# A hybrid decoder layer on one core: where weight rests, block sums of the merged tensor and filler products stand

## The chip, the core and the metric

The kernel runs on one core of a Trainium2 chip. The engines are TensorE (PE, with its weight loads as PEld), VectorE (DVE), ScalarE (ACT), GpSimd (POOL) and SyncE (SP), which issues the transfers. The metric is the device time of one execution in microseconds (us), as the median of several runs. Besides it there is one profiled execution, from which all rows below come; a row's first number is its start, counted from the start of the span.

## The reference

One layer with two token mixers side by side, 1024 tokens, width 1024, float32:

```python
h = rms_norm(x, norm_w); proj = h @ w_in          # 7440 columns, split into 11 pieces
o_a = sliding_window_attention(rope(q), rope(k), v, sinks) * silu(a_gate)   # 16 heads, window 128
y_a = o_a @ w_a_proj
o_b = rms_norm(gated_linear_attention(b_q, b_k, b_v, log_a)) * silu(b_gate) # 4 heads, chunks
y_b = o_b @ w_b_proj
merged = sigmoid(m_a) * y_a + sigmoid(m_b) * y_b
out = rms_norm(x + merged @ w_out, final_norm_w)
```

## The kernel before

Every large product is taken with both factors split in two: a high part, rounded to TensorE's fp32r format by a copy on ScalarE, and a rest, which is the raw value minus the high part. `split_w` (L114 to L116) does it for weights, the rest on GpSimd (tiles `wl`), and `split_block` (L904 to L906) for blocks of 128x512 of an activation, the rest on VectorE or GpSimd. A product is then three matmuls: high by high, rest by high, high by rest. `half_product` (its matmuls have the line L132) takes 4 x 3 = 12 of them, 128x512 each; `token_product` (L420) the same with 256 columns.

Several projections are taken as 2x2 block products with seven products instead of eight (`seven_products`): four sums of weight blocks, four sums of activation blocks (`t1` to `t4`), seven products and seven sums of results. In the results, `u` is product 1 copied from PSUM by ScalarE, and each later product is added to it from PSUM by VectorE (L451, L459 and their neighbours). It serves three places: the pairs of projections with `w_in`, the four sets with `w_b_proj`, whose results are merged at once with `y_a` and the gates (`merge`), and the output projection with `w_out`, in two halves.

In order of time the span has these stages. The input norm and the transposes (0 to about 110 us). The pairs of projections with `w_in` (110 to 408). The window attention (408 to 728). It has more work for TensorE than its own, and at its end three "fillers" are put, `m_tiles`, each a projection tile of one of the gates, 48 matmuls of 128x512. The linear attention of heads 0 and 1 (728 to 798, `gla(0)`), a chain of small steps (`gla_step`, 16 of them) in which the engines wait for each other; between the steps stand matmuls of one more filler, spread by the list `pace`, which says behind which step each third matmul may stand. The linear attention of heads 2 and 3 with the products for `y_a` between its steps in the same manner (798 to 888). The blocks of `o_b` (`block_sums`, then the two last ones) and the four sets with `w_b_proj` (from about 882 to 990). The blocks of `merged`, all in one `block_sums` behind the last merge, with the splits of blocks 0, 1, 4, 5 and 6 on GpSimd and those of 2 and 3 on VectorE (990 to 1030). Then the output projection, the residual, the final norm and the stores.

The order of the instructions on each engine is not written out. A scheduler that simulates the program's timeline sets it, under the dependencies, the buffers in each pool and the limits of `pace`. A pool is a region of SBUF that opens where the code opens it; `vr`, `vh` and `vl` are a linear attention step's values and their two parts, in the pool `hpv`, which opens behind the window attention. Transfers stand in the queue of SP in program order as the scheduler gives it, and a transfer that waits for a buffer holds up those behind it. The rotation of queries and keys exchanges halves by such transfers (`qs`).

Of the kernel before, what the change touches and what calls it, by code (L numbers as in the profile page):

```python
# [25 lines left out]
P = 128  # L26
# [43 lines left out]
def layer_kernel(ctx: ExitStack, tc: tile.TileContext, consts, x, positions, norm_w, w_in, a_sinks,  # L70
# [42 lines left out]

    def split_w(raw, h, l):  # L114
        nc.scalar.copy(h, raw)  # L115
        nc.gpsimd.tensor_sub(l, raw, h.bitcast(F32))  # L116
# [10 lines left out]
    def half_product(p, w, m, start, stop):  # L127

        for k in range(4):
            with tc.issue_after(pace.pop(0)) if pace else nullcontext():  # L130
                for y, (a, b) in enumerate(((w[0], m[0]), (w[0], m[1]), (w[1], m[0]))):
                    nc.tensor.matmul(p, a[:, k, :], b[:, k, :], start=start and k == 0 and y == 0,  # L132
                                     stop=stop and k == 3 and y == 2)
# [282 lines left out]
    def token_product(p, w, m, t):  # L416

        for k in range(4):
            for y, (i, j) in enumerate(((0, 0), (1, 0), (0, 1))):
                nc.tensor.matmul(p, m[i][:, k, t * P : t * P + P], w[j][:, k, :], start=k == 0 and y == 0,  # L420
                                 stop=k == 3 and y == 2)

    def seven_products(raw, tset, n, u_pool, dest, emit, early=None, fine=False):
# [6 lines left out]
        nb = n // P  # L430

        def product(raw, m):
            w = part(raw, n)
            x = [bank("sj") for b in range(nb)]
            for b in range(nb):
                if n == P:
                    half_product(x[b], w, m, True, True)
                else:
                    for t in range(2):
                        token_product(x[b][:, t * 256 : t * 256 + 256], w, m, 2 * b + t)  # L440
            return x
# [4 lines left out]
        def like(p, o):  # L446
            return p.rearrange("p (t c) -> p t c", t=2) if len(o.shape) == 3 else p

        def add(o, u, x):
            for b in range(nb):  # L450
                nc.vector.tensor_add(o[b], like(u[b], o[b]), like(x[b], o[b]))  # L451

        def earlier(u, a, th):
            for b in range(nb):
                if early:
                    early(u[b], a, th, b)

        def give(a, th, u, x):
            o = [dest(a, th, b) for b in range(nb)]  # L459
            for b in range(nb):  # L460
                nc.vector.tensor_add(o[b], like(u[b], o[b]), like(x[b], o[b]))
                emit(o[b], a, th, b)

        x = product(a11, b11)
        u = tiles("u")
        for b in range(nb):
            nc.scalar.copy(u[b], x[b])  # L467
        x = product(a12, b21)
        c = [dest(0, 0, b) for b in range(nb)]
        add(c, u, x)  # L470
        earlier(c, 0, 0)
        for b in range(nb):
            emit(c[b], 0, 0, b)
        x = product(a22, t4)
        c = [dest(1, 0, b) for b in range(nb)]
        for b in range(nb):
            nc.scalar.copy(c[b], like(x[b], c[b]))
        earlier(c, 1, 0)
        nc.vector.tensor_add(a22, a21, a22)
        nc.vector.tensor_sub(a21, a11, a21)  # L480
        nc.vector.tensor_sub(a11, a22, a11)
        nc.vector.tensor_sub(a12, a12, a11)
        add(u, u, product(a11, t2))
        u3 = tiles("u3")
        add(u3, u, product(a21, t3))
        for b in range(nb):
            nc.vector.tensor_add(c[b], c[b], like(u3[b], c[b]))
            emit(c[b], 1, 0, b)
        x = product(a22, t1)
        add(u, u, x)  # L490
        earlier(u3, 1, 1)
        give(1, 1, u3, x)
        earlier(u, 0, 1)
        if not fine:
            give(0, 1, u, product(a12, b22))
            return
        w = part(a12, n)
        for b in range(nb):
# [569 lines left out]
```

## Time and profile before

| | |
|---|---|
| median of three runs | 1111.57 us (1110.83 to 1113.48) |
| profiled execution, own time | 1108.61 us |
| its span | 1106.7 us |
| mean granted TensorE clock | 0.979 |
| PE busy | 1027.7 us, 93% |
| PEld busy | 873.9 us, 79% |
| DVE busy | 774.7 us, 70% |
| ACT busy | 542.4 us, 49% |
| POOL busy | 684.3 us, 62% |

Busy time is the time in which an instruction runs, and a share is over the whole span; stages with different limits are mixed in it. A row of the chain of waits is a start, a length and what filled it. In a row of stretches stand the length, then busy time and count of instructions for PE, PEld, DVE, ACT and POOL, then the granted clock, the share of DMA and GB/s. A row of groups has the line, engine, operation, result and inputs, count, busy time and mean ns of one, and the idle time ahead of it with what ended it.

### The profile page before, as it was taken

The page shows a single profiled execution, that of the slowest core. Times are in us where ns is not written, and L with a number is a line of the kernel's source. Part 1 is how long each engine was busy: PE and PEld are TensorE (multiplying, and loading weights), DVE is VectorE, ACT ScalarE, POOL GpSimd, SP SyncE. Part 2 cuts the span into 40 slices and gives each one's busy share as a digit, 9 for nine tenths or more (in the row PEclk, how much of TensorE's full clock was granted, in tenths as well). Part 3 has the DMA queues.
Part 4 walks back from the last instruction along what each step waited for, and adds up shares of the span by engine and source line. Part 5 has one row for each costly group of instructions (what it writes and reads, how often), then busy time and mean ns, then how long its engine had stood idle before and what let it go on. Part 6 is the DMA issues. An engine that isn't in the chain of part 4 may idle for free.

```text
span 1106.7 us, 16321 instructions
## 1 busy us (share of the span) xinstructions
PE 1027.7 (93%) x5544; PEld 873.9 (79%) x5544; DVE 774.7 (70%) x1241; ACT 542.4 (49%) x1312; POOL 684.3 (62%) x542
## 2 busy tenths in 40 slices
PE   4999999899999999999999999988999997994896
PEld 3786787688889997888888878777788886873896
DVE  5999887335564323489788788748755299899766
ACT  6345865333342214556666666557654143243444
POOL 6033555777985446578677567747744246688685
PEclk9999999999999999999999999989999998996999
DMA  7332443452424152222222124266644587531315
GB/s 256 87 114 68 144 160 119 142 188 95 131 98 127 65 153 60 65 69 68 68 83 78 49 77 132 82 206 206 219 148 152 194 253 238 171 115 57 124 50 190
DMA packets 126403, 141.07 MB, mean 127 GB/s; under 512 B 10352, under 2 KB 87024, under 8 KB 126320
## 3 DMA queue, kind: packets, MB, share of 16 engines
q1 hardware_dynamic: 126320, 140.03, 40.5%
q8 instruction: 44, 0.72, 0.3%
q14 instruction: 39, 0.32, 0.1%
HBM read 95.04 MB, written 40.24 MB: 122 GB/s over the span
## 4 chain that ended last, share of the span: by engine, by line
PE 60%; DVE 16%; POOL 8%; issue 6%; ACT 6%; DMA 4%; SPq 1%; POOLq 0%; DVEq 0%; ACTq 0%
PE pj L132 22%; PE sj L132 15%; PE sj L420 11%; POOL wl L116 3%; PE sc L689 2%; PE av L729 2%; PE av L774 2%; POOL b L906 2%; DMA r<-sp_ob 1%; POOL o L906 1%; ACT wh L115 1%; PE pt L713 1%; PE sc L774 1%; DVE u L523 1%; DMA gt<-sp_cum 1%
## 5 line engine op out<-in xcount | busy, mean ns | idle before, releaser
L132 PE MATMUL pj<-o,wh 128*128 128x512 f32 x1088 | 353.6, 400 | 2.5 <-ACT o L204 1.9
L132 PEld LDWEIGHTS pj<-o,wh 128*128 128x128 f32 x1088 | 200.8, 190 | 44.2 <-ACT o L204 2.1
L116 POOL TENSOR_TENSOR wl<-wr,wh 128x1024 fp32r<-128x1024 f32 (+1 forms) x76 | 167.4, 2211 | 107.5 <-ACT wh L115 99.7
L116 POOL TENSOR_TENSOR wl<-sraw,wh 128x512 fp32r<-128x512 f32 (+1 forms) x98 | 155.3, 1600 | 107.6 <-ACT wh L115 105.5
L132 PE MATMUL pj<-o,wl 128*128 128x512 f32 x544 | 215.6, 396 | 0.0
L132 PEld LDWEIGHTS pj<-o,wl 128*128 128x128 f32 x544 | 102.5, 188 | 21.6
L115 ACT CAST wh<-wr 128x1024 fp32r<-128x1024 f32 (+1 forms) x76 | 66.9, 890 | 93.3 <-PE pj L132 23.9
L132 PE MATMUL sj<-o,wh 128*128 128x512 f32 x352 | 110.5, 395 | 0.7 <-ACT u L467 0.7
L451 DVE TENSOR_TENSOR u<-u,sj 128x512 f32<-128x512 f32 x72 | 49.2, 683 | 72.0 <-PE sj L420 40.5
L115 ACT CAST wh<-sraw 128x512 fp32r<-128x512 f32 (+1 forms) x98 | 63.2, 678 | 57.2 <-PE sj L420 29.1
L420 PE MATMUL sj<-wh,b 128*128 128x256 f32 x320 | 62.2, 296 | 21.7 <-ACT b L905 14.7
L132 PEld LDWEIGHTS sj<-o,wh 128*128 128x128 f32 x352 | 65.9, 187 | 16.9 <-ACT u L467 1.1
L420 PEld LDWEIGHTS sj<-wh,b 128*128 128x128 f32 x320 | 52.8, 203 | 23.1 <-ACT b L905 15.1
L132 PE MATMUL sj<-o,wl 128*128 128x512 f32 x176 | 69.4, 394 | 0.0
L721 POOL TENSOR_TENSOR ch<-ph,cst 128x512 fp32r<-128x512 f32 x32 | 38.4, 1201 | 48.4 <-ACT ph L720 36.0
L704 ACT ACTIVATE sm<-sc,nm 128x129 f32<-128x129 f32 x128 | 45.8, 368 | 37.4 <-DVE nm L700 36.4
L132 PE MATMUL sj<-b,wh 128*128 128x512 f32 x160 | 51.0, 402 | 5.6 <-ACT wh L115 5.6
L420 PE MATMUL sj<-wh,o 128*128 128x256 f32 x320 | 55.2, 277 | 0.1
L420 PEld LDWEIGHTS sj<-wh,o 128*128 128x128 f32 x320 | 48.4, 188 | 0.4 <-ACT wh L115 0.3
L420 PE MATMUL sj<-wl,b 128*128 128x256 f32 x160 | 45.8, 293 | 0.2 <-POOL wl L116 0.2
L609 POOL TENSOR_TENSOR qs<-qs,sin 128x512 f32<-128x512 f32 x18 | 25.4, 1409 | 31.0 <-DMA qs<-q 31.0
L420 PE MATMUL sj<-wl,o 128*128 128x256 f32 x160 | 44.3, 277 | 0.0
(314 smaller groups left out, 2737.3 us busy)
## 6 DMA issues: line engine op xcount, KB each, us to landing
sraw<-in_w_in_dram SPq DMA_DIRECT2D x32, 512.0 KB, 4.0
wr<-in_w_in_dram SPq DMA_DIRECT2D x26, 512.0 KB, 4.0
r<-sp_ob SPq DMA_DIRECT2D x28, 256.0 KB, 4.3
qs<-q SPq DMA_DIRECT2D x72, 64.0 KB, 2.0
xt<-in_x_dram SPq DMA_DIRECT2D x8, 512.0 KB, 8.6
sp_ma<-gt SPq DMA_DIRECT2D x16, 256.0 KB, 2.0
sp_mb<-c SPq DMA_DIRECT2D x16, 256.0 KB, 2.0
gt<-sp_cum SPq DMA_DIRECT2D x16, 256.0 KB, 3.7
```

Source lines behind the costliest of these rows:

```text
L115: nc.scalar.copy(h, raw)
L116: nc.gpsimd.tensor_sub(l, raw, h.bitcast(F32))
L132: nc.tensor.matmul(p, a[:, k, :], b[:, k, :], start=start and k == 0 and y == 0, stop=stop and k == 3 and y == 2)
L420: nc.tensor.matmul(p, m[i][:, k, t * P : t * P + P], w[j][:, k, :], start=k == 0 and y == 0, stop=k == 3 and y == 2)
L451: nc.vector.tensor_add(o[b], like(u[b], o[b]), like(x[b], o[b]))
L609: nc.gpsimd.tensor_mul(qs, qs, sin[:, sl])
L689: nc.tensor.matmul(s[:, h * 256 : h * 256 + 256], lq, kk[kv][x][:, k0 : k0 + 2, :].rearrange("p n t -> p (n t)"), start=x == 0, stop=x == 1)
L704: nc.scalar.activation(sm[:, j, :], sel[j // 2][:, j % 2, :], AF.Exp, bias=nm[:, j : j + 1], accum_out=den[:, j : j + 1])
L721: nc.gpsimd.tensor_mul(ch, ph.bitcast(F32), leb)
L729: nc.tensor.matmul(av[:, b * 256 : b * 256 + 256], val[:, blk, kv, :], part[:, 2 * b : 2 * b + 2, :], start=y == 0, stop=y == len(terms) - 1)
L774: nc.tensor.matmul(p, a[i], b[j], start=start and y == 0, stop=stop and y == 2)
L906: (eng or nc.vector).tensor_sub(m[1][:, k, :], r, f(m, 0, k))
```

## The change

1. `split_w` takes its engine from a list, `rest`. It is GpSimd as before until the first three tiles of `y_a`, and VectorE from there on.
2. `seven_products` is written anew. Weight parts of products 1, 2 and 6 and the sums of weights stand at its start, later weight parts ahead of the product that uses them. Without `order` (the pairs with `w_in`) the sums are as before, and product 6 is copied to a tile of its own. With `order`, products 3 and 5 are accumulated on product 1's bank in PSUM and product 7 on product 4's, with copies of the bank in between on ScalarE (`u1`, `u3`, `u5`); VectorE then adds four times per block instead of seven.
3. The pool `hpv` opens ahead of the window attention. Two of the fillers stand at the attention's end instead of three, two in the linear attention's first half instead of one, and `pace` lets six of their matmuls stand behind each step instead of three.
4. `block_sums` is gone. The first five blocks of `o_b` are taken row by row ahead of the later `y_a` tiles, the last two behind products of the first set with `w_b_proj`. The differences of `merged` are taken for the first three of its four rows behind each set, and the splits stand behind the products of the last set. All of this is on VectorE.
5. In the output projection the two halves of `w_out`'s rows are exchanged, the order of the products is (1, 2, 4, 6, 3, 5, 7) in the first half and (1, 2, 6, 3, 5, 4, 7) in the second, the residual is added behind the sum for three of four blocks, and the multiplication by the final norm's weights goes from GpSimd to VectorE.

```diff
+    rest = [nc.gpsimd]
     def split_w(raw, h, l):
         nc.scalar.copy(h, raw)
-        nc.gpsimd.tensor_sub(l, raw, h.bitcast(F32))
+        rest[0].tensor_sub(l, raw, h.bitcast(F32))
...
-    def seven_products(raw, tset, n, u_pool, dest, emit, early=None, fine=False):
+    def seven_products(raw, tset, n, u_pool, dest, emit, order=None, early=None, fine=False, after=None):
...
+        w = {i: part(r, n) for i, r in ((1, a11), (2, a12), (6, a22))}
         nc.vector.tensor_add(a22, a21, a22)
         nc.vector.tensor_sub(a21, a11, a21)
         nc.vector.tensor_sub(a11, a22, a11)
         nc.vector.tensor_sub(a12, a12, a11)
...
+        for i in order:
+            ahead(i)
+            x[i] = x[{3: 1, 5: 1, 7: 4}[i]] if i in (3, 5, 7) else [bank("sj") for b in range(nb)]
...
+            for b in range(nb):
+                product(i, b)
+            if i in (1, 3, 5):
+                u[i] = [u_pool.tile([P, 512], F32, name=f"u{i}") for b in range(nb)]
+                for b in range(nb):
+                    nc.scalar.copy(u[i][b], x[i][b])
...
+            if i == 2:
+                give(0, 0, 1, 2)
+            if i in (4, 5) and 4 in x and 5 in u:
+                give(1, 1, 5, 4)
+            if i in (5, 6) and 6 in x and 5 in u:
+                give(1, 0, 5, 6)
+            if i == 7:
+                give(0, 1, 3, 7)
+            if after:
+                after(i)
...
+    c3 = ExitStack()
+    hpv = c3.enter_context(pool_of(name="hpv", bufs=4))
     with ExitStack() as c2:
...
-                for _ in range(3):
+                for _ in range(2):
                     m_tiles([fillers.pop(0)])
...
-    pace += [steps[min(15, 2 + i)] for i in range(16 * len(fillers))]
+    pace += [steps[min(15, 2 + i // 2)] for i in range(16 * len(fillers))]
...
     ya_tiles((0, 1, 2))
+    rest[0] = nc.vector
...
+    def sum_row(k):
+        t1s.append(c21[3] if k == 3 else rp.tile([P, 512], F32, name="r"))
+        t2s.append(rp.tile([P, 512], F32, name="r"))
+        nc.vector.tensor_sub(t1s[k], c22[k], c21[k])
+        if k < 3:
+            less_row(k)
+
+    def less_row(k):
+        nc.vector.tensor_sub(t2s[k], c12[k], t1s[k])
+        nc.vector.tensor_sub(c22[k], c12[k], c22[k])
+
+    def sums(i):
+        y = {1: 0, 2: 1, 3: 3, 4: 5, 5: 4, 6: 2, 7: 6}[i]
+        mt[y] = block(y)
+        rows = {0: c21, 1: c11, 2: c11, 3: t2s, 4: c22, 5: t1s}
+        if i < 7:
+            for k in range(4 if i == 2 else 3):
+                split_block(mt[y], k, rows[y][k])
...
         seven_products([[r[:, 4 * i : 4 * i + 4, :] for r in w] for i in range(2)], ob, P, up_,
-                       lambda a, th, b: mg[a][th][:, k, :], merge)
+                       lambda a, th, b: mg[a][th][:, k, :], merge, range(1, 8), after={0: last_blocks, 3: sums}.get(k))
+        if k < 3:
+            sum_row(k)
...
-    mt = blocks() + last_blocks()
-    block_sums(mt, [(k, [mg[i][th][:, k, :] for i in range(2) for th in range(TH)]) for k in range(4)], zw, (0, 1, 4, 5, 6))
...
-            nc.sync.dma_start(w[i, a], w_out[i * 512 : i * 512 + 512, c : c + 256].rearrange("(k p) c -> p k c", p=P))
+            nc.sync.dma_start(w[i, a], w_out[512 - i * 512 : 1024 - i * 512, c : c + 256].rearrange("(k p) c -> p k c", p=P))
...
-                    nc.gpsimd.tensor_mul(o[:, t, :], o[:, t, :], fnw[:, cs])
+                    nc.vector.tensor_mul(o[:, t, :], o[:, t, :], fnw[:, cs])
```

The scheduler makes of it another order on the engines. In the first place below, TensorE's rows before, between two steps of the linear attention's heads 0 and 1, `pj` is the filler, L813 to L815 are a step's first three products, and `sc` is the update of a state.

```order
L847 MATMUL pt<-cst,on 128x128 x2
L813 MATMUL av<-bq,bk 128x64
L814 MATMUL av<-bq,bk 64x64
L815 MATMUL av<-cst,kp 128x128
L132 MATMUL pj<-o_83,wh 128x512
L132 MATMUL pj<-o_84,wh 128x512
L132 MATMUL pj<-o_83,wl 128x512
L774 MATMUL sc<-vh,kth 128x256
```

Three filler matmuls stand between the first products of a step and its next ones. The same place on TensorE now, where L850 to L852 are a step's first products and the row behind the fillers is its inner product with the values:

```order
L884 MATMUL pt<-cst,on 128x128 x2
L850 MATMUL av<-bq,bk 128x64
L851 MATMUL av<-bq,bk 64x64
L852 MATMUL av<-cst,kp 128x128
L134 MATMUL pj<-o_85,wh 128x512
L134 MATMUL pj<-o_86,wh 128x512
L134 MATMUL pj<-o_85,wl 128x512
L134 MATMUL pj<-o_85,wh 128x512
L134 MATMUL pj<-o_86,wh 128x512
L134 MATMUL pj<-o_85,wl 128x512
L811 MATMUL av<-vh,ath 128x256
```

Three more filler matmuls have come into the gap; they stood at the window attention's end. The second place is GpSimd before, at the blocks of `merged` (`o_9494` to `o_9497` are the quarters of `merged`, the `b_` and the other `o_` tiles the parts of its blocks, `wl` weight rests):

```order
L906 TENSOR_TENSOR b_10123<-o_9494,b_10122 128x512 x3
L906 TENSOR_TENSOR b_10125<-o_9496,b_10124 128x512 x3
L906 TENSOR_TENSOR b_10123<-o_9494,b_10122 128x512
L116 TENSOR_TENSOR wl<-wr,wh 128x1024 x2
L906 TENSOR_TENSOR b_10131<-o_9495,b_10130 128x512 x3
L906 TENSOR_TENSOR o_10133<-o_9494,o_10132 128x512 x3
L906 TENSOR_TENSOR b_10125<-o_9496,b_10124 128x512
L116 TENSOR_TENSOR wl<-wr,wh 128x1024
L906 TENSOR_TENSOR o_10135<-o_9497,o_10134 128x512 x4
L906 TENSOR_TENSOR o_10133<-o_9494,o_10132 128x512
L906 TENSOR_TENSOR b_10131<-o_9495,b_10130 128x512
L116 TENSOR_TENSOR wl<-wr,wh 128x1024 x3
```

GpSimd did the rests of five blocks (L906) and weight rests of `w_out` (L116) in one piece here, behind the last weight rests of `w_b_proj`. Now no row of these stands on GpSimd, which has nothing between the linear attention's last rows and the sums of the final norm. The third place is VectorE now, in the last of the four sets with `w_b_proj` (L459 adds out of PSUM, L1052 and L1053 are the merge, L940 is a block's rest, L439 and L440 are sums of weights, L118 a weight rest):

```order
L459 TENSOR_TENSOR o_9468<-u_9925,sj 128x512
L459 TENSOR_TENSOR o_9467<-u_9925,sj 128x512
L118 TENSOR_TENSOR wl<-wr,wh 128x512
L439 TENSOR_TENSOR wr<-wr 128x512
L1052 SCALAR_TENSOR_TENSOR o_9468<-ym,o_9468 128x512
L1052 SCALAR_TENSOR_TENSOR o_9467<-ym,o_9467 128x512
L940 TENSOR_TENSOR b_10014<-o_9467,b_10013 128x512
L440 TENSOR_TENSOR wr<-wr 128x512
L940 TENSOR_TENSOR b_10014<-o_9467,b_10013 128x512
L459 TENSOR_TENSOR o_9465<-u_10011,sj 128x512
L1053 TENSOR_TENSOR o_9468<-o_9468,yt 128x512
L118 TENSOR_TENSOR wl<-wr,wh 128x512
```

Rests of `merged`'s blocks and weight rests now stand between the merges, in VectorE's own queue.

238 lines of the change are left out of this document (129 added, 109 removed).

## The prediction

> **What bounds the kernel now.** I read four views in this order: the chain of waits, the busy time by stretches, what TensorE waited for, and the timeline of the last stages. The chain first (start, length, what; all in us):
>
> ```profile
> 715.24 5.60 PE pj L132 x24
> ...
> 728.50 5.25 DMA vr<-sp_bv
> ...
> 775.00 4.88 DMA oraw<-sp_oa
> ...
> 1031.84 4.58 POOL wl L116
> 1036.46 47.41 PE sj L420 x398
> ```
>
> Outside a few places the chain is TensorE at its own pace: 24 matmuls of 512 columns take 5.60 us (0.233 us each), and 398 of 256 columns 47.41 us (0.119 us each). The places where it leaves TensorE are a value load at the start of the linear attention (728.50) and VectorE and GpSimd work before the output projection. The stretches show how much each is worth (length, then busy time and count of PE, PEld, DVE, ACT, POOL, granted clock, DMA):
>
> ```profile
> 711.00:728.00 17.00, 16.80 (x90) 13.67 (x90) 6.61 (x18) 8.60 (x22) 8.27 (x6) 1.00 0.32 109
> 728.00:798.40 70.40, 59.56 (x349) 50.27 (x348) 53.38 (x135) 45.55 (x144) 52.02 (x70) 0.93 0.69 222
> 798.40:888.60 90.20, 90.20 (x488) 75.61 (x487) 44.92 (x115) 38.50 (x107) 35.17 (x47) 1.00 0.54 173
> 888.60:990.30 101.70, 96.06 (x409) 77.93 (x409) 93.92 (x111) 38.80 (x66) 61.52 (x39) 0.97 0.64 200
> 990.30:1096.00 105.70, 83.67 (x661) 81.96 (x660) 83.40 (x93) 43.97 (x99) 82.81 (x59) 0.90 0.27 88
> ```
>
> TensorE idles 10.8 us in the linear attention's first half (728 to 798.4), nothing after it, 5.6 us in the products with w_b_proj, 22.0 us from the output projection's first matmul to the last one, and 10.7 us are behind its last matmul (1096 to 1106.7). What lies ahead of 711 keeps its order on TensorE. What it waits for in the third stage:
>
> ```profile
> PE sj L420 <- ACT b L905: 14.7, 2, 12.6
> ...
> PE sj L132 <- ACT wh L115: 5.6, 1, 5.6
> ```
>
> ACT L905 is the rounding of merged's blocks, which itself waits for VectorE. So the bound from 882 to 1032 is VectorE, and these stretches show how:
>
> ```profile
> 882.00:919.40 37.40, 31.83 (x138) 25.40 (x136) 36.58 (x49) 17.78 (x32) 14.97 (x9) 0.97 0.85 275
> 919.40:975.00 55.60, 55.54 (x234) 45.34 (x235) 48.64 (x61) 17.43 (x32) 34.31 (x22) 0.96 0.61 180
> 975.00:1019.40 44.40, 25.93 (x143) 22.27 (x142) 43.99 (x30) 17.32 (x30) 44.40 (x25) 0.85 0.26 89
> 1019.40:1032.00 12.60, 9.38 (x54) 8.97 (x54) 12.46 (x18) 5.01 (x8) 0.21 (x2) 0.77 0.01 2
> ```
>
> VectorE is busy 141.7 of 150.0 us. But with GpSimd busy all the time (975 to 1019.4) it does 30 instructions in 44 us, 1.47 us each; with GpSimd idle (1019.4 to 1032) 18 in 12.5 us, although four of these are twice as wide. Single rows say the same:
>
> ```profile
> 882.80 0.69 DVE L917 TENSOR_TENSOR r<-r 128x512 f32<-128x512 f32 x1
> 883.41 0.68 DVE L906 TENSOR_TENSOR b<-r,b 128x512 fp32r<-128x512 f32 x1
> ...
> 885.21 0.68 DVE L920 TENSOR_TENSOR r<-r,t 128x512 f32<-128x512 f32 x1
> ...
> 1009.88 1.75 DVE L917 TENSOR_TENSOR o<-o,o 128x512 f32<-128x512 f32 x1
> 1011.55 1.75 DVE L920 TENSOR_TENSOR o<-o,t 128x512 f32<-128x512 f32 x1
> ...
> 1028.80 0.68 DVE L906 TENSOR_TENSOR b<-o,b 128x512 fp32r<-128x512 f32 x1
> 1029.40 1.22 DVE L481 TENSOR_TENSOR wr<-wr 128x1024 f32<-128x1024 f32 x1
> 1030.54 1.27 DVE L451 TENSOR_TENSOR o<-u,sj 128x512 f32<-128x512 f32 x2
> ```
>
> ```profile
> 1009.37 8.40 POOL L906 TENSOR_TENSOR o<-o,o 128x512 fp32r<-128x512 f32 x5
> ```
>
> From 882.80 to 885.21 four instructions of 128x512 go by, one per 0.603 us (the next starts before the last one's 0.68 are over); at 1009.88, beside GpSimd's five, the same L917 takes 1.75. One of 128x1024 takes 1.14 us from start to start (1029.40 to 1030.54).
>
> **The change part by part.** (1) Linear attention: values early, a second filler. Today TensorE is full up to 728 (16.80 of 17.00) and then lacks work. One filler is 48 matmuls at 0.233 = 11.2 us; it leaves the full stretch and goes between the steps (six filler matmuls a step instead of three, 1.4 instead of 0.7 us, in the rows of the order shown with the change), and eight values are loaded and four of them split at about 410 us instead of 728, so that the wait at 728.50 (5.25 us) goes. All work is the same; what can be won is the idle time, 10.8 us, and a part of what the clock of 0.93 costs on 59.6 us (up to 4 us, if it comes from the gaps). Against all of it stands that VectorE is busy 53.38 of 70.40 us there and would have to do that in some 60, and that the load of 4.88 us at 775.00, on which ScalarE stands, stays. I take 10 us; bounds 0 and 14.
>
> (2) Differences and splits, VectorE alone. By the order of the changed kernel, from the first split of o_b to the last split of merged VectorE executes 191 instructions of 128x512 (56 splits, 28 weight rests, 16 adds out of PSUM, 32 merges, 16 + 4 differences of o_b, 16 of weights, 16 of merged, 7 others) and 9 of 128x1024. GpSimd, whose rows of the order are shown with the change, has none beside them. At the spacings above: 191 x 0.603 + 9 x 1.14 = 125.4 us. Before, the same stretch runs from VectorE's first L906 at 882.07 to the end of the last at 1029.48 (1028.80 + 0.68): 147.4 us, 8.3 of them idle in the four stretches. With the same idle time the new one takes 133.7, a gain of 13.7. This is longer than TensorE's own work of that stretch, so VectorE stays the bound, by less.
>
> ```profile
> 882.07 0.69 DVE L906 TENSOR_TENSOR b<-r,b 128x512 fp32r<-128x512 f32 x1 [3.72 <-ACT b L905]
> ```
>
> Behind the last split today TensorE needs 66.5 us to its last matmul at 1096, since it then still waits for GpSimd's 4.58 us of weights (1031.84). In the new order the split that comes last (t4, product 6) is followed by 11 products of 48 matmuls at 0.119 = 62.8 us, and their weights are split: 3.7 us more. Together 17.4 us. Bounds: without any idle time on VectorE 25.7; at the 0.69 us that a row lasts rather than 0.603, 191 x 0.69 + 9 x 1.22 + 8.3 = 151.1 us, and nothing is left (3.7 lost and 3.7 won).
>
> (3) Sums in PSUM. Three of seven adds fall away per product set (12 in the stretch, already left out of the 191), one more copy on ScalarE comes, at 38.80 of 101.7 us busy without weight. Products 3, 5 and 7 now wait until their bank was copied or read; product 2, 4 or 6 runs meanwhile (12 x 0.233 = 2.8 us, or 5.7 in the output projection), longer than a copy and an add: 0, and up to 2 us each where VectorE is late, which the idle time of (2) holds.
>
> (4) Weights ahead in the earlier products. On TensorE, ScalarE and GpSimd the order up to the attention differs only in names (a copy of product 6 goes to a tile of its own): 0, bounds -2 and 2.
>
> (5) Eight value loads and four splits at the attention's start. The loads go to SP's queue ahead of the exchanges for the rotation, and some of them wait for GpSimd's splits of the first, 25.9 / 32 = 0.81 us each by the group of these splits, so the exchanges stand behind them. Behind that group's row stands one from GpSimd's timeline at the attention's start:
>
> ```profile
> L769 POOL TENSOR_TENSOR vl<-vr,vh 128x256 fp32r<-128x256 f32 x32 | 25.9, 814 | 20.2 <-ACT vh L768 20.2
> ```
>
> ```profile
> 418.01 1.29 POOL L609 TENSOR_TENSOR qs<-qs,sin 128x512 f32<-128x512 f32 x1 [6.95 <-DMA qs<-q]
> ```
>
> GpSimd is idle 6.95 us there, which covers its four splits (3.3 us); the queue may be late by 1 to 3 us, and behind it stands the key path. I take a loss of 1, bounds 0 and 4.
>
> (6) The end. The multiplications by the norm's weights (24 of 128x256) and the weight rests go to VectorE: by the order it then has, from the last split of merged on, some 30 rows of 128x512 at 0.603, 14 of 128x1024 at 1.14 and 40 of 128x256 at 0.3 to 0.4 (half a 512's and its start), about 50 us under some 63 of TensorE, so TensorE stays the bound. The last 10.7 us (add, square, sum, reciprocal root on GpSimd, two multiplications, store) keep their steps: 0, bounds -2 and 2.
>
> **The rivals.** (a) VectorE's price is the row's length, 0.69, not the spacing: (2) gives nothing, 1106.7 - 10 + 1 = 1097.7. For it: chains of dependent instructions could not overlap; against it: the rows from 882.80 depend on each other in part and are still 0.603 apart. [...]
>
> (b) The linear attention gains nothing: it is bound by its chain over ScalarE, VectorE and GpSimd (45.55, 53.38 and 52.02 of 70.40), and the filler only fills the waits: then the 11.2 us that left the stretch before 728 are won and lost again in the steps, and the span is 1106.7 - 17.4 + 1 = 1090.3.
>
> (c) TensorE alone bounds: (1) 14, (2) 25.7, (5) 0: 1106.7 - 39.7 = 1067.
>
> (d) The slower one: VectorE's instructions are slow for another reason than GpSimd, such as the loads (DMA share 0.85 at 882), and keep the mean of 882 to 1019.4, 129.2 us / 140 = 0.92 us. Now that the weights and all splits stand in its queue, the stretch takes 191 x 0.92 + 9 x 1.74 + 8.3 = 199.7 us, 52.3 more: 1106.7 + 52.3 - 3.7 - 10 + 1 = 1146.3. It decides from 0.73 us per instruction on, where the loss in (2) eats the other gains. Against it: at 882.80 the loads are at their densest and the rows 0.603 apart. [...]
>
> **How the numbers follow.** 1106.7 - 10 - 17.4 + 1 = 1080.3 us of span. The median of the runs, 1111.57, stands 4.9 above the span of the profiled execution (its own time, 1108.61, 1.9 above it): 1085.2. With 4.9 on each: (a) 1102.6, (b) 1095.2, (c) 1071.9, (d) 1151.2. Chances: forecast 0.60, (a) 0.10, (b) 0.12, (c) 0.14, (d) 0.04. The forecast's own bounds, two terms at their ends at once being rare, are 1074 to 1097; to leave out no more than 2 in 10 the range takes in most of (c) and (a): 1068 to 1102. A measurement of this kernel tells 0.3%, 3.3 us, from no change: faster 0.93, same 0.03 (between (a) and (d)), slower 0.04.
>
> **What would show it.** After: GpSimd nearly empty from the first o_b split to the norm, VectorE rows of 128x512 at 0.6 to 0.7 us there and none at 1.7; that stretch 126 to 140 us long; no TensorE wait over 5 us at the output projection's start, and the granted clock near 1 there; TensorE's idle time in the linear attention's first half below 3 us, with no value load in the chain. It is wrong if VectorE's rows stay above 0.8 us, if idle time on it between 882 and the output projection grows beyond some 20 us (loads of merged's inputs or SP's queue late), or if the attention's start loses more than 4 us to the early values.

## The result

The changed kernel takes 1083.62 us in the median of four runs (1080.67 to 1085.99), the kernel before 1111.20 (four runs, 1110.33 to 1113.48): a ratio of 0.9747, 95% interval 0.9715 to 0.9779. The profiled execution of the changed kernel took 1085.99 us, the slowest of the four, with a span of 1084.2 and a granted clock of 0.988. A second set of runs gave 0.9734 (0.9709 to 0.9760), a median of 1081.58 and a profiled span of 1080.0.

The stretches of the changed kernel, cut where VectorE's first split of o_b begins (879.3), its last split of merged ends (1014.4) and the last matmul begins (1075.2); the columns are those of the stretches before:

```profile
711.00:728.00 17.00, 15.50 (x87) 12.34 (x86) 13.70 (x28) 6.59 (x19) 13.74 (x12) 1.00 0.30 98
728.00:798.40 70.40, 64.23 (x384) 54.31 (x382) 54.30 (x135) 49.07 (x150) 51.93 (x68) 0.98 0.76 246
798.40:879.30 80.90, 80.90 (x447) 68.05 (x446) 41.40 (x111) 33.82 (x98) 18.70 (x39) 1.00 0.47 151
879.30:1014.40 135.10, 126.00 (x613) 104.79 (x612) 126.94 (x202) 59.64 (x102) 0.00 (x0) 0.99 0.55 176
1014.40:1075.20 60.80, 60.21 (x510) 60.02 (x508) 46.26 (x83) 31.08 (x83) 3.73 (x10) 1.00 0.37 119
1075.20:1084.20 9.00, 0.26 (x3) 0.05 (x1) 3.46 (x11) 3.58 (x8) 3.48 (x7) 0.69 0.69 255
```

The same cuts in the kernel before:

```profile
882.10:1029.50 147.40, 120.11 (x553) 99.43 (x551) 139.14 (x152) 56.26 (x96) 93.72 (x55) 0.92 0.52 164
1029.50:1097.30 67.80, 67.42 (x555) 67.01 (x556) 45.64 (x64) 31.55 (x80) 54.45 (x43) 0.97 0.36 117
1097.30:1106.70 9.40, 0.31 (x3) 0.12 (x2) 3.87 (x14) 4.04 (x10) 3.22 (x8) 0.71 0.60 223
```

From the first split of o_b to the last of merged VectorE now does 202 instructions instead of 152 (the counts of these rows) in 12.3 us less, and GpSimd none instead of 55. A single instruction shows why. VectorE's timeline of the changed kernel at the end of that stretch:

```profile
1005.51 0.67 DVE L1011 TENSOR_TENSOR o<-o,o 128x512 f32<-128x512 f32 x1
1006.12 0.68 DVE L940 TENSOR_TENSOR o<-o,o 128x512 fp32r<-128x512 f32 x1
1006.72 1.21 DVE L439 TENSOR_TENSOR wr<-wr 128x1024 f32<-128x1024 f32 x1
...
1013.73 0.68 DVE L940 TENSOR_TENSOR b<-o,b 128x512 fp32r<-128x512 f32 x1
```

Nothing lasts 1.7 us there any more, and 128x512 follow each other by 0.60 us. Its chain of waits goes over to TensorE behind that:

```profile
1003.85 1.13 DVE wl L118
1006.79 1.13 DVE wr L439
1008.59 60.54 PE sj L422 x508
```

The 508 matmuls run without a break up to 1069.1; what the path holds behind them are the last adds and the final norm. What was lost stands at the other end, and the waits of TensorE show it (all of the program, longest first after the input norm's):

```profile
PE pt L684 <- ACT q L681: 4.2, 1, 4.2
...
PE sj L134 <- ACT wh L117: 0.9, 1, 0.9
```

The first of them, 4.2 us, is at the start of the window attention; before it was 0.9.

For the comparison of all runs I read four places out of each profiled execution: the first score product of the attention, VectorE's first split of o_b, the end of its last split of merged, and the start of the last matmul. Between them lie the stages (us; the first column is a point in time, the others lengths):

| kernel | first score | to first o_b split | to last split of merged | to last matmul | behind it | span |
|---|---|---|---|---|---|---|
| before | 456.3 | 425.8 | 147.4 | 67.8 | 9.4 | 1106.7 |
| changed | 463.0 | 416.3 | 135.1 | 60.8 | 9.0 | 1084.2 |
| changed, again | 461.6 | 411.4 | 137.3 | 60.8 | 9.0 | 1080.0 |
| late values | 457.9 | 411.0 | 136.2 | 60.8 | 9.0 | 1074.8 |
| values back | 457.9 | 426.6 | 132.9 | 66.0 | 9.1 | 1092.5 |
| one filler | 461.8 | 403.7 | 140.0 | 62.2 | 9.1 | 1076.7 |
| rests on GpSimd | 462.8 | 408.6 | 146.4 | 65.7 | 9.1 | 1092.6 |
| GpSimd twice | 460.7 | 406.3 | 155.6 | 62.2 | 9.1 | 1093.9 |
| sums at the end | 460.7 | 411.0 | 135.4 | 61.0 | 9.1 | 1077.2 |
| no accumulation | 462.9 | 412.9 | 141.1 | 67.5 | 8.9 | 1093.4 |
| late values, one filler | 457.2 | 413.7 | 136.1 | 60.8 | 9.0 | 1076.9 |
| the same, sums at the end | 456.6 | 411.2 | 138.7 | 60.8 | 9.0 | 1076.3 |
| before, late values | 457.6 | 415.0 | 150.6 | 68.2 | 9.0 | 1100.4 |
| before, all on VectorE | 457.1 | 428.8 | 145.4 | 62.5 | 9.8 | 1103.7 |

The two executions of the changed kernel differ by 4.9 us between the first score product and o_b. The variants whose edit lies at its end or behind it (rests on GpSimd, GpSimd twice, sums at the end, no accumulation) stand between 406.3 and 412.9. So the column is good to some 5 us only, and smaller differences are read from the medians.

### The profile page after: what moved, and what is told of

Same layout as the page of the kernel before. It is cut to its first block, busy times and chain, and to the rows that moved or that the text cites. A ratio compares the mean times of both kernels' runs of the same rounds, so it can differ in the third digit from the quotient of the medians.

```text
span 1084.2 us, 16205 instructions
## 1 busy us (share of the span) xinstructions
PE 1024.2 (94%) x5544; PEld 870.5 (80%) x5544; DVE 766.2 (71%) x1312; ACT 546.5 (50%) x1320; POOL 528.5 (49%) x447
## 4 chain that ended last, share of the span: by engine, by line
PE 56%; DVE 19%; POOL 7%; issue 6%; ACT 5%; DMA 5%; SPq 1%; POOLq 0%; DVEq 0%; ACTq 0%
PE pj L134 18%; PE sj L134 18%; PE sj L422 13%; POOL wl L118 2%; PE av L811 1%; PE av L767 1%; DVE qb L708 1%; DVE qa L707 1%; PE sc L727 1%; DVE b L940 1%; DVE sc L735 1%; DVE sm L750 1%; DMA r<-sp_ob 1%; ACT sm L742 1%; DVE nm L738 1%
## 5 line engine op out<-in xcount | busy, mean ns | idle before, releaser
L134 PEld LDWEIGHTS pj<-o,wh 128*128 128x128 f32 x1088 | 203.4, 192 | 44.1 <-ACT o L206 2.1
L118 POOL TENSOR_TENSOR wl<-sraw,wh 128x512 fp32r<-128x512 f32 (+1 forms) x98 | 156.3, 1612 | 108.0 <-ACT wh L117 105.1
L146 POOL TENSOR_SCALAR rstd<-zs 128x1 f32<-128x1 f32 x8 | 2.7, 335 | 210.6 <-DVE zs L1072 210.2
L118 POOL TENSOR_TENSOR wl<-wr,wh 128x1024 fp32r<-128x1024 f32 x29 | 72.4, 2497 | 35.1 <-ACT wh L117 29.4
L476 DVE TENSOR_TENSOR u<-u,sj 128x512 f32<-128x512 f32 x48 | 32.9, 685 | 55.8 <-PE sj L422 32.5
L422 PE MATMUL sj<-wh,b 128*128 128x256 f32 x320 | 59.8, 288 | 5.0 <-DVE b L940 3.6
L459 DVE TENSOR_TENSOR c<-u,sj 128x512 f32<-128x512 f32 x48 | 32.7, 681 | 27.7 <-DMA sp_bg<-c 8.4
L118 DVE TENSOR_TENSOR wl<-wr,wh 128x512 fp32r<-128x512 f32 (+1 forms) x47 | 41.7, 899 | 9.1 <-ACT wh L117 8.9
```

Source lines behind the costliest of these rows:

```text
L118: rest[0].tensor_sub(l, raw, h.bitcast(F32))
L459: nc.vector.tensor_add(o, like(u[i][b], o), like(x[j][b], o))
L476: nc.vector.tensor_add(o[b], u[i][b], x[j][b])
```

## The experiments

### The early values

The theory: the eight value loads at the attention's start hold up SP's queue, and the early values, not the second filler, make the linear attention shorter. Three runs take the parts asunder, and the changed kernel went with them on the same chip.

> The changed kernel once more, on the chip of the other three runs, as their yardstick: ratio to the kernel before 0.972 to 0.978, span 1082 to 1086 us.

Measured: 1081.58 (0.9734), with a span of 1080.0 a little below the expected one. Beside it, the loads spread:

```diff
+            stores.append(nc.sync.dma_start(sp_oa[...], oa).ins)          # window attention
...
+        with tc.issue_after(stores[4 + 2 * t + hd]) if hd < 2 and t < 4 else nullcontext():
             nc.sync.dma_start(vr, sp_bv[t * P : t * P + P, hd * BV : (hd + 1) * BV])
```

> The eight early value loads are queued behind stores of the window attention, one behind each of eight of them, instead of standing at the attention's start. Theory: these loads held the first exchange of the rotation on SP's queue from 413.81 (before) to 417.85 us (after), so TensorE waited 4.2 us for ScalarE's q and then ran at a granted clock of 0.50 for 5 us; with the loads spread the exchange starts at 413 to 415 again, TensorE has no wait over 1.5 us between 425 and 445, and 5 to 6.5 us are won: span 1078 to 1079. Rival: the loss is of the pool's place or of the seven products rewritten, and the loads only happen to stand there: within 1 us of the changed kernel.

Measured: 1075.30 us (1074.24 to 1076.93), ratio 0.9683 (0.9658 to 0.9707), 6.3 us below the changed kernel on the same chip, with no overlap of their runs. SP's queue at the attention's start, before:

```profile
413.81 8.77 SPq L608 DMA_DIRECT2D qs<-q  x8
```

in the changed kernel:

```profile
410.32 1.98 SPq L857 DMA_DIRECT2D vr<-sp_bv  x2
...
416.10 1.71 SPq L857 DMA_DIRECT2D vr<-sp_bv  x3
417.85 2.75 SPq L646 DMA_DIRECT2D qs<-q  x4
```

and with the loads spread:

```profile
415.37 8.77 SPq L647 DMA_DIRECT2D qs<-q  x8
```

GpSimd's timeline of the changed kernel has the first splits here:

```profile
415.33 2.83 POOL L806 TENSOR_TENSOR vl<-vr,vh 128x256 fp32r<-128x256 f32 x4 [3.30 <-ACT vh L805]
```

The fifth to seventh value load (416.10) waited for a buffer, that is for these splits, and the exchange behind them started 4.0 us later than before. Of these, 1.0 us had been lost ahead of this place: the rounding of weights on ScalarE in front of it starts at 408.51 instead of 407.54. The chain of waits shows what the splits themselves had waited for:

```profile
408.46 6.37 DMA vr<-sp_bv
...
417.49 0.32 SPq L857
417.85 0.62 SPq L646
```

The first load takes 6.37 us, more than the four splits. And a second queue is held as long. The exchange sends `q`, which ScalarE copies from PSUM, and in ScalarE's order this copy stands behind the high parts of the early values. ScalarE's timeline now, and the same copy before:

```profile
414.85 0.75 ACT L805 CAST vh<-vr 128x256 fp32r<-128x256 f32 x2 [5.29 <-DMA vr<-sp_bv]
416.23 0.77 ACT L805 CAST vh<-vr 128x256 fp32r<-128x256 f32 x2 [0.63 <-DMA vr<-sp_bv]
416.91 0.58 ACT L642 COPY q<-pj 128x512 f32<-128x512 f32 x1
```

```profile
413.20 0.59 ACT L604 COPY q<-pj 128x512 f32<-128x512 f32 x1 [4.61 <-PE pj L132]
```

The copy ends at 417.49, so with SP's queue free the exchange could have started only 0.4 us sooner. What this made of TensorE, in two stretches of the changed kernel and of the one with the loads spread:

```profile
430.00:435.00 5.00, 0.94 (x5) 0.41 (x3) 4.34 (x4) 1.57 (x3) 3.06 (x2) 0.86 0.08 24
435.00:440.00 5.00, 4.82 (x14) 3.96 (x15) 3.34 (x5) 4.83 (x9) 1.13 (x1) 0.50 0.00 0
```

```profile
430.00:435.00 5.00, 4.11 (x20) 3.09 (x19) 3.53 (x5) 3.11 (x6) 0.37 (x1) 1.00 0.00 0
435.00:440.00 5.00, 5.00 (x25) 4.06 (x24) 1.43 (x3) 2.39 (x5) 3.88 (x3) 1.00 0.06 11
```

TensorE stood still for 4.2 us and then, at a granted clock of 0.50, did 14 matmuls in 5 us, where the other kernel did 25. That the early loads cost this is shown, in size too (5 to 6.5 us expected, 6.3 measured); the wait left is 0.9 us, as before. Through which queue they do is not: with the loads spread both are free, and ScalarE copies `q` at 414.76. The exchange at 415.37 is a little later than expected, since the pairs ended 1.5 us later in this kernel.

The pool back behind the attention, the loads with it:

```diff
-    hpv = c3.enter_context(pool_of(name="hpv", bufs=4))     # ahead of the attention
...
+    hpa, bp1, bpe, bps, hpv, bp, hp = (...)                 # behind it, as before
```

> The changed kernel with the pool of the values opened behind the window attention as before, and two fillers in the linear attention's first half. Theory: the attention's start wins 5 to 6 us, and the linear attention loses 3 to 5 of them, because its first steps wait for a value load (5.25 us in the chain of before) and for GpSimd's splits: span 1081 to 1084. Rival: the early values do nothing for the linear attention, the second filler does it all: span 1078 to 1079.

Measured: 1094.01 (0.9853), 12.4 us slower than the changed kernel; both numbers missed. The attention's start came back (first score at 457.9), but the linear attention lost far more than the expected 3 to 5. Its chain of waits says where:

```profile
723.85 2.02 DMA sp_oa<-oa
...
726.95 4.60 DMA vr<-sp_bv
731.57 0.41 ACT vh L804
```

and TensorE's waits from 695 to 800:

```profile
PE av L810 <- ACT vh L804: 11.2, 1, 11.2
```

The value load follows the attention's last store, in time and in SP's queue; without the third filler in front TensorE has nothing to do meanwhile and waits 11.2 us for the high part of the values. In the kernel before the same wait was 4.1 us, with one filler more ahead of it:

```profile
PE av L774 <- ACT vh L768: 4.1, 1, 4.1
```

So the early load and the moved filler belong together: with the filler moved, the early values are worth 12.4 us net of what they cost at the attention's start. By the table not all of this lies in the linear attention: the output projection is 5.2 us longer too, of which the stretch ahead of it makes up 2.2 to 4.4.

The fillers as before, the early values kept:

```diff
-                for _ in range(2):
+                for _ in range(3):
                     m_tiles([fillers.pop(0)])
...
-    pace += [steps[min(15, 2 + i // 2)] for i in range(16 * len(fillers))]
+    pace += [steps[min(15, 2 + i)] for i in range(16 * len(fillers))]
```

> The changed kernel with three fillers at the attention's end and one between the steps of heads 0 and 1, as before; the early values stay. Theory: the second filler, 11.2 us of TensorE's work, fills idle time between the steps; without it TensorE's idle time from 728 to 798 goes from 6 to about 10 us and the granted clock falls again: 4 to 8 us slower than the changed kernel, span 1088 to 1092. Rival (b) of the prediction: the steps' chain is the bound and a filler costs there what it saves ahead: within 2 us of the changed kernel.

Measured: 1078.71 (1076.06 to 1078.81), ratio 0.9704 (0.9675 to 0.9734): not slower, but 2.9 us faster than the changed kernel, with overlapping intervals. The theory is out, and the rival's 2 us are passed by a little. The same two stretches as above, of this kernel:

```profile
711.00:728.00 17.00, 17.00 (x94) 14.24 (x92) 7.62 (x18) 8.48 (x23) 8.09 (x6) 1.00 0.40 133
728.00:798.40 70.40, 64.53 (x401) 55.38 (x400) 57.25 (x154) 48.40 (x157) 51.75 (x73) 0.95 0.80 252
```

From 728 to 798.4 TensorE idles 5.9 us with one filler in the steps and 6.2 in the changed kernel, where some 10 were expected. The filler kept ahead of the steps fills 711 to 728, which the changed kernel leaves at 15.50 of 17.00. In these 87.4 us TensorE does 495 matmuls by the rows; the changed kernel does 471 and in its second execution 485, so more than half of that difference is one between executions.

The early values alone, on the kernel before, loads spread:

> The kernel before with the values' pool ahead of the window attention and the eight loads spread behind stores of the attention; one filler between the steps as before. Theory: the early values alone win what the linear attention won, 9 to 10 us, and nothing is lost at the attention's start: 1100 to 1102. Rival: without the rest of the change the time is given back to VectorE's stretch behind it: 1105 to 1110.

Measured: 1102.03 (1101.79 to 1102.76), ratio 0.9911 (0.9895 to 0.9928): 9.1 us faster. The first o_b split comes 9.5 us earlier than before (872.6 by the sum of the first two columns). A small part is given back behind it, where VectorE's stretch takes 150.6 instead of 147.4. The theory holds.

### VectorE and GpSimd

The theory: GpSimd's instructions take VectorE's time, so VectorE alone is faster although it has more to do. Two runs, one with GpSimd's share of the weight rests put back, one with VectorE's work unchanged and GpSimd busy for nothing:

```diff
-    rest[0] = nc.vector
```

> The changed kernel, but all weight rests stay on GpSimd. Theory: GpSimd's instructions take VectorE's time, whatever they compute. In the stretch from the first split of o_b to the last of merged (135.1 us in the changed kernel) GpSimd then has 28 rests of 128x512 at about 1.6 us and 9 of 128x1024 at 2.4, 67 us, in which VectorE does one instruction per 1.47 us (46 of them), and the other 117 at 0.603 take 71 us: with 8 us idle 146 us, 8 to 12 us slower than the changed kernel although VectorE has 27 us less to do. Rival: only the length of VectorE's queue counts, so that with 27 us less in it TensorE bounds: 3 to 8 us faster.

Measured: 1094.50 (0.9847), 12.9 us slower than the changed kernel's second set (another chip; there the ratio was 0.9734), and the stretch took 146.4 us, where 146 were expected:

```profile
871.50:1017.90 146.40, 126.57 (x579) 105.28 (x577) 135.12 (x168) 58.67 (x102) 70.79 (x34) 0.94 0.51 160
```
The rival (a shorter queue of VectorE is faster) is out: VectorE had 34 instructions fewer there and needed 9 to 11 us more. TensorE's waits in the output projection name a second cost, GpSimd's slow weight rests themselves:

```profile
PE sj L422 <- POOL wl L118: 9.7, 2, 5.3
```

The other run takes two SBUF inputs on GpSimd beside each of VectorE's weight rests (the subtraction's result is read by nobody):

```diff
         rest[0].tensor_sub(l, raw, h.bitcast(F32))
+        if rest[0] is nc.vector:
+            ...
+                nc.gpsimd.tensor_sub(d, x.bitcast(F32), x.bitcast(F32))    # 128x448, into a scratch tile
```

> The changed kernel with VectorE doing all it does there, and beside each weight rest from the later y_a tiles on one or two subtractions of 128x448 on GpSimd whose result nobody reads. Theory (GpSimd's instructions take VectorE's time): some 46 of them in the stretch at 1.5 us are 69 us, in which VectorE does 47 instructions instead of 114: 25 to 40 us slower than the changed kernel. Rival (VectorE's 1.75 us of before had another cause, loads or dependences): within 3 us, since nothing waits for GpSimd.

Measured: 1098.92 (0.9887, 0.9856 to 0.9917), 17.3 us slower by medians, and the stretch 155.6 us instead of 135.1 and 137.3 (the row is cut 0.1 us later):

```profile
867.00:1022.70 155.70, 135.57 (x633) 109.03 (x632) 151.93 (x204) 60.93 (x103) 65.90 (x44) 0.96 0.50 156
```
Nobody reads what they compute. In the stretch one thing waits for them, a rounding on ScalarE that overwrites the tile they read, for 2.0 us at 1018.42 (two more such waits stand outside it). So it is their presence that costs: VectorE is busy 151.93 us instead of 126.94, with 204 instructions instead of 202. VectorE's and GpSimd's timeline of this kernel, side by side:

```profile
926.30 0.68 DVE L465 TENSOR_TENSOR o<-u,sj 128x512 f32<-128x512 f32 x1
926.89 0.82 DVE L1058 SCALAR_TENSOR_TENSOR o<-ym,o 128x512 f32<-128x512 f32 x1
927.64 1.42 DVE L446 TENSOR_TENSOR wr<-wr 128x512 f32<-128x512 f32 x1
928.98 1.42 DVE L118 TENSOR_TENSOR wl<-wr,wh 128x512 fp32r<-128x512 f32 x1
...
936.15 0.67 DVE L465 TENSOR_TENSOR o<-u,sj 128x512 f32<-128x512 f32 x1
...
938.09 0.68 DVE L1059 TENSOR_TENSOR o<-o,yt 128x512 f32<-128x512 f32 x1
```

```profile
925.97 7.90 POOL L124 TENSOR_TENSOR dm<-wh 128x448 f32<-128x448 f32 x6 [7.00 <-ACT wh L117]
935.72 1.30 POOL L124 TENSOR_TENSOR dm<-wh 128x448 f32<-128x448 f32 x1 [1.85 <-ACT wh L117]
```

Beside GpSimd's six an instruction with both inputs in SBUF takes up to 1.42 us (0.82 at 926.89, where GpSimd's first one is nearly over by their mean of 1.32 us), and 0.68 when they are gone; the adds out of PSUM at 926.30 and 936.15 take 0.68 and 0.67 beside GpSimd too. The direction is the expected one, the size two thirds of the least that was expected (25 to 40). The expectation priced every VectorE instruction beside GpSimd at 1.47 us, though the adds out of PSUM took 0.67 and 0.68 us beside it, and VectorE's idle time took a part: by the rows of the stretch it fell from 8.2 to 3.8 us.

The move alone, on the kernel before (weight rests from the later y_a tiles on, all blocks' rests and the final norm's multiplications on VectorE, in the old order):

```diff
     ya_tiles((0, 1, 2))
+    rest[0] = nc.vector
...
-        block_sums(ob, ..., rp, (3,))
+        block_sums(ob, ..., rp, ())
...
-    block_sums(mt, ..., zw, (0, 1, 4, 5, 6))
+    block_sums(mt, ..., zw, ())
...
-                    nc.gpsimd.tensor_mul(o[:, t, :], o[:, t, :], fnw[:, cs])
+                    nc.vector.tensor_mul(o[:, t, :], o[:, t, :], fnw[:, cs])
```

> The kernel before with one part of the change alone: weight rests from the later y_a tiles on, all blocks' rests and the multiplications by the final norm's weights on VectorE; sums in their old order and places. Theory by counts of instructions: 201 of 128x512 at 0.603, 9 of 128x1024 at 1.14 and 11 us idle are 142.5 us for the stretch of 147.4, and the 4.6 us of GpSimd's weights behind it go: 1101 to 1104. Rival by what the runs left out of the changed kernel: without the move it lost 13 us, so the move alone wins about that: 1096 to 1100. Second rival: in the old order all blocks of merged wait in one queue behind the last merge, and the move alone wins nothing: 1107 to 1113.

Measured: 1105.29 (0.9934, 0.9908 to 0.9959), 5.9 us faster, a little short of the count's 1101 to 1104; both rivals miss. Behind the last split TensorE took 62.5 us instead of 67.8, as expected without GpSimd's weights. The stretch won only 2.0 of the expected 4.9 us:

```profile
885.90:1031.30 145.40, 125.26 (x576) 103.79 (x575) 132.61 (x210) 57.47 (x98) 0.00 (x0) 0.93 0.55 173
```

VectorE is busy 132.6 us, near the count's 131.5, and idle 12.8 where 11 were expected; what the idle time comes from is not shown. One wait of TensorE there is long:

```profile
PE sj L134 <- ACT wh L117: 6.9, 1, 6.9
```

The first set of products waits for its weights, but the kernel before had 5.6 us of this wait too. The changed kernel, which takes weight parts ahead, has 0.9. What taking them ahead is worth alone was not run.

### The places of the sums, and the accumulation

All differences and splits of merged behind the last set, on VectorE:

```diff
-                       ..., merge, range(1, 8), after={0: last_blocks, 3: sums}.get(k))
-        if k < 3:
-            sum_row(k)
+                       ..., merge, range(1, 8), after={0: last_blocks}.get(k))
+    for k in range(3):
+        sum_row(k)
+    for i in range(1, 8):
+        sums(i)
```

> The changed kernel, but all differences and splits of merged stand behind the last of the four sets, on VectorE, in the order of the products that read them. Theory: VectorE's number of instructions bounds the stretch, not their places, and the output projection starts with the first blocks while the others are split: 0 to 4 us slower. Rival: the interleaving is the gain, and 44 instructions at 0.603 us (27 us) come behind the last merge, with TensorE's first two products ahead of them: 10 to 20 us slower.

Measured: 1080.24 (0.9726, 0.9691 to 0.9762) beside 0.9734 of the changed kernel: no difference. The stretch takes 135.4 us and holds the same 202 instructions of VectorE. So interleaving them is worth nothing that can be measured here. On the faster base it is the same:

> The spread loads, one filler, and all differences and splits of merged behind the last set. If the places of these instructions among the products are worth nothing, as their count bounds the stretch: within 2 us of the same kernel with the sums interleaved. Rival: with less work ahead VectorE is the bound for longer, and the interleaving pays now: 3 to 8 us slower.

Measured: 1077.54 (0.9690, 0.9676 to 0.9704) beside 1077.53 with the sums interleaved.

Each product in its own bank, with VectorE's adds as before:

```diff
-            x[i] = x[{3: 1, 5: 1, 7: 4}[i]] if i in (3, 5, 7) else [bank("sj") for b in range(nb)]
+            x[i] = [bank("sj") for b in range(nb)]
...
-                    nc.scalar.copy(u[i][b], x[i][b])
+                        nc.vector.tensor_add(u[i][b], u[i - 2][b], x[i][b])       # i in (3, 5)
...
-                       (1, 2, 6, 3, 5, 4, 7) if h else (1, 2, 4, 6, 3, 5, 7), early=residual, fine=h == 1)
+                       (1, 2, 6, 3, 5, 4, 7), early=residual, fine=h == 1)
```

The last lines give the output projection's first half the order of products of the second.

> The changed kernel with each product in a bank of its own, sums by VectorE as before (three more adds per set, two copies fewer on ScalarE), and the order (1, 2, 6, 3, 5, 4, 7) in both halves of the output projection. Theory: VectorE bounds the stretch, so 12 more adds of 0.69 us there cost 5 to 8 us, and nothing in the output projection, where VectorE has 46 of 61 us to do. Rival: the accumulation costs as much in waits for the bank as it saves: within 2 us.

Measured: 1092.27 (0.9831, 0.9797 to 0.9866), 10.7 us slower. The stretch took 141.1 us, 4 to 6 more than the changed kernel's two, which fits the expected 5 to 8 at its lower end. The other 6.7 us lie in the output projection and are this edit's own: with the sum of products 3 and 4 on VectorE, the residual can only be added behind it, and the last half's residual is loaded late. TensorE's waits there:

```profile
PE sj L422 <- DVE u L522: 4.3, 1, 4.3
PE sj L422 <- DVE o L544: 4.3, 1, 4.3
```

So this run does not price the accumulation in the output projection.

### The two faster edits together

> The changed kernel with both edits that made it faster: the early value loads spread behind stores of the window attention, and three fillers at the attention's end with one between the steps. If the two gains are of different places (6.3 us at the attention's start, 2.9 between the steps) they add up: median 1071 to 1073.5. Rival: the one filler was only better by chance of the order, or because the late exchange shifted the steps: 1074 to 1077, as with the spread loads alone.

Measured: 1077.53 (1076.76 to 1078.67), ratio 0.9691 (0.9676 to 0.9706). They do not add up (1071 to 1073.5 expected): it is the same as the spread loads alone (0.9683, interval 0.9658 to 0.9707). The filler's place makes no difference that can be told, in either kernel. The spread loads are the version that beats both kernels, by 0.6% over the changed one.

## Why the prediction was right, step by step

By spans the steps add up to the measured 22.5 us of the first execution, from the table: 6.7 lost up to the first score, 9.5 won to o_b, 12.3 in VectorE's stretch, 7.0 behind it, 0.4 at the end.

(1) Linear attention, 10 forecast (bounds 0 and 14): 9.5 and 14.4 in the two executions by the table. On TensorE alone, from the first score product to the first matmul with `w_b_proj`, it is 7.1 and 12.1 (432.4 us before, 425.3 and 420.3). The size was right, half of the reason was wrong. The early values alone gave 9.1 us on the kernel before. The second filler gave nothing: rival (b) is true of it, though not of the whole step. TensorE still idles 6.2 us between 728 and 798.4 (3.7 in the second execution), where below 3 was given as the sign; no value load stands in the chain there.

(2) VectorE alone, a stretch of 133.7 us forecast: 135.1 and 137.3. The count (191 of 128x512 and 9 of 128x1024 by the trace as by the order; the row's 202 takes in two that lie over its ends), the spacing of 0.603 and the idle time of 8.3 (8.2, and 10.5 in the second execution) all held. By rival (a), 0.69 an instruction, it would have been 151; (d), 0.92, is out. The runs with GpSimd busy show the cause that was named: 146.4 us with 34 instructions fewer. Behind the last split 62.8 were forecast, 60.8 measured. There the prediction read the time before wrongly: TensorE's last matmul starts at 1097.3 and not at 1096, so that 67.8 us stood there instead of 66.5, and 7.0 were won instead of 3.7.

(3) The adds saved were in the count of (2), and nothing further was forecast. The 4 to 6 us in the stretch without the accumulation fit 12 adds at 0.603 (7.2) less some idle time.

(4) Forecast 0: the first score stands at 456.6 to 457.9 in the four kernels with the rewritten products and no value loads at the attention's start, at 457.1 and 457.6 in the two built on the kernel before, and at 456.3 in the kernel before itself. No loss over 1.6 us shows there, as forecast.

(5) The attention's start, a loss of 1 forecast with bounds 0 and 4: this step failed. The prediction wrote that GpSimd's 6.95 us of idle time covered its four splits, and that the queue may be late by 1 to 3 us. The splits were covered, but the step has neither the first load's 6.37 us ahead of them nor ScalarE, which copies `q` behind the early values' high parts. The exchange was 4.0 us late, 3.1 without what had been lost ahead of it, so the delay itself was nearly the 3 us named. Taking a loss of only 1 for it was wrong: TensorE's wait grew from 0.9 to 4.2 us, and to it came a clock of 0.50, which the prediction had not priced. In all it cost 3.7 and 5.1 us by the first score against the spread loads' 457.9, 6.3 by medians. Over 4 us was among the signs given for being wrong, and it occurred.

(6) TensorE bounds the output projection (60.21 of 60.80 us busy, VectorE 46.26), as forecast; the end kept its length (9.4 and 9.0).

In sum 26.4 us of span were forecast, 22.5 and 26.7 measured. The median came out at 1083.6 against 1085.2 partly by luck: the forecast span, 1080.3, was 3.9 too low for the first execution, and the 4.9 us added from span to median were too many, since the medians of the changed kernel's two sets stand 0.6 below and 1.6 above their profiled spans.

Not every part has a run of its own. On the kernel before, the early values won 9.1 us and the move to VectorE 5.9, together 15.0 of the 27.6 by medians. The weights taken ahead, and in the output projection the exchanged halves and the order of products, were not run alone.

## What to carry to other kernels

Price an engine's queue by instructions times the spacing that its rows show while its neighbour is idle (0.603 us here), and look up separately what they take beside the neighbour (up to 1.42 us a row): moving work onto the busier of two engines can pay where the other's instructions lengthen its own, as here, where VectorE was busy 151.93 us with GpSimd's unread subtractions and 126.94 without. A load that is made early must also be followed through the queue it is issued from and through the engine that reads it: here the value loads waited for a buffer, the exchange behind them started at 417.85 instead of 413.81 us, and ScalarE's copy of `q`, behind the high parts of the values, at 416.91 instead of 413.20. Here a few lines that hang each load behind a later transfer gave the gain without the loss. Where VectorE's count of instructions bounded a stretch here, their order within it made no difference that could be told, and neither did the place of a filler.

## What the runs showed of the hardware

With a short stop of TensorE more than its length was lost here: the kernel with the loads spread, which lacks it, was 6.3 us faster by medians. After 4.2 us of waiting the granted clock was 0.50 from 435 to 440 us, and 14 matmuls went by instead of 25. By slices of a microsecond it was 1.00 up to 433, 0.50 from 434 to 440 and 1.00 again from 441. The kernel before has the same at its value load, with a wait of 4.1 us: 0.50 from 733 to 739 and 1.00 from 740. How long a stop has to be for this was not shown.

Of VectorE's rows of 128x512 here, GpSimd slowed some that read both inputs from SBUF: up to 1.42 us beside its unread subtractions and 0.67 to 0.69 without, in the timelines from 925 to 940 and from 1000 to 1014.5 us. The adds out of PSUM kept 0.67 to 0.68 there (926.30, 936.15 and 1000.92). Not every row beside GpSimd was slowed: those at 1000.32, 1011.16 and 1011.76 took 0.68 each, while rows of GpSimd of 3.93 us (two subtractions, from 999.74) and 8.32 us (one, from 1009.06) were open. Over whole stretches VectorE lost 0.46 us per us of GpSimd's work with the rests on GpSimd and 0.37 with the unread subtractions (its busy time less its instructions, 163 and 4 or 191 and 11, at 0.603 and 1.14, over GpSimd's 70.8 and 65.9 us). Why the two rates differ is not settled.

Executions of the same order differ. The changed kernel's two and those of four of its variants (rests on GpSimd, GpSimd twice, sums at the end, no accumulation) have one order on TensorE through the window attention, and took 259.4 to 265.0 us from the first score product to the last product with the attention's values; the first execution of the changed kernel is the longest. No run here shows what from.
